# A hybrid trunk kernel on one core: S5 in stages between the weight chunks, GpSimd's work on other engines, a convolution that reads PSUM

## The chip, the cores and the metric

The kernel runs on one core of a Trainium2 chip. The metric is the device time of one execution in microseconds, lower is better. The engines are called TensorE (PE in the rows; PEld is its weight load), VectorE (DVE), ScalarE (ACT), GpSimd (POOL) and SyncE (SP). Before the change three runs took 1272.61, 1277.6 and 1278.52 us.

## What is computed

Two layers over 272 tokens (16 learned ones and 256 of the input) of width 1024. In each, one projection feeds four parallel causal mixers of width 512, whose outputs are merged by gates and followed by a squared-ReLU MLP:

```python
for l in range(DEPTH):
    proj = rms_norm(h, norm_pre_mix[l]) @ w_in[l]
    # retention (rotary q, k), S5, SSD (with a causal convolution of 4 taps), HGRN2
    y_ret, y_s5, y_ssd, y_hg = mixers(split(proj))
    mixed = sum(sigmoid(gate_n) * (y_n @ w_branch[l, n])) @ w_out[l]
    h = h + rms_norm(mixed, norm_post_mix[l])
    m = square(relu(rms_norm(h, norm_pre_mlp[l]) @ w_up[l])) @ w_down[l]
    h = h + rms_norm(m, norm_post_mlp[l])
```

The S5 mixer, with complex state of 64 for each of 32 groups of 16 channels:

```python
x_t = ab * x_{t-1} + bb @ u_t                 # complex, diagonal ab
y = gelu(real(c @ x) + d_skip * u)            # 512 channels
a, gt = split(y @ glu_w + glu_b); out = a * sigmoid(gt)
```

## The kernel before

Activations lie with channels on the partitions and tokens along the row (272 wide; the second layer's last parts 256). All large weights come as 336 chunks of 128x1024 in the order of `ORDER`, 168 a layer. `chunk` takes the next one: SyncE loads it into `wst`, ScalarE rounds it to `whi` (L325), VectorE makes the rest `wlo` (L327). `gemm` gives 24 matmuls a chunk: whi by the high half of the activation (L344), whi by its low half (L345), wlo by the high half (L347), into PSUM banks `g` (three). The other PSUM banks are `ma`, `mb` (two each) and `mc` (one).

Each engine works through its queue in order. The order is made before the run by a planner that simulates the program with times of its own and gives each engine the ready instruction of the highest priority: program order, moved ahead inside `high_priority` (a chunk's two halves by 400 places). `issue_after(x)` queues what is traced inside it behind x on x's engine.

A layer's order: HGRN2's projections (chunks 0 to 11) and its attention, the SSD's convolution inputs (12 to 19) and attention, S5's input (20 to 23), then the gates and branches: HGRN2's gate (24), gates (28), SSD's gate z (36), HGRN2's branch (40), SSD's gates (44), the rotary q and k (52), v (56), SSD's branch (60), retention's gate (64), two sets of gates (68), the GLU of S5 (84), two branches (88), the output projection (96), the MLP (104).

S5 runs in four blocks of 128 channels. For each, `s5_prep` loads 256 KB (`s5a`), builds the input matrices (`s5g`) and two output matrices (`s5b` on VectorE, `s5c` on GpSimd) by products of 512 elements (L1011 to L1013), and a table of powers (`s5e`, `s5_table`, six products of 288 elements on GpSimd). TensorE makes the direct term with 32-wide weights over 128 columns (`kd`, L1042 and L1043) and turns the input matrices (`bt`). `s5_run` multiplies by 128-wide weights over 68 columns (L1109), scales (L1115 to L1120), runs two recurrences (L1128), scales back (L1132 to L1137), multiplies again (L1143, L1146) and adds the skip term (L1139, L1148). After each second block `s5_out` applies the activation and puts rows in their places with 16 copies of 32 partitions on ScalarE and VectorE (L1160, L1162). Every S5 tile has one buffer.

`ret_in` copies q and k out of PSUM, loads the rotary tables `rot`, and lets GpSimd form four products of 32 partitions (L1496), one of 128 (L1497) and two sums. `hgrn_in` forms the forget gate on VectorE (L1201) and the key on GpSimd (L1202). In `ssd_in` the convolution copies a chunk to SBUF and then does three multiply-adds on VectorE (L1405).

Of the kernel before, what the change touches and what calls it, by code (L numbers as in the profile page):

```python
# [9 lines left out]
F32 = mybir.dt.float32  # L10
# [223 lines left out]
class Net:  # L234
    def __init__(self, ctx, tc, io, dbg=None):
# [170 lines left out]
    def layer(self, l):  # L406
# [45 lines left out]
        s5y = self.s5(l, self.s5_in(l, u_all))  # L452
# [17 lines left out]
        s5y = self.glu(l, s5y, (8, 2), sl)  # L470
# [306 lines left out]
    def scalars(self):  # L777
# [55 lines left out]
    def s5_params(self):  # L833
# [89 lines left out]
        cmul(*P(3), *P(2), *P(1))  # L923
        cmul(*P(4), *P(2), *P(2))
# [18 lines left out]
        for s in (2, 1, 0):  # L943
            cmul(c5[:, 0, s], c5[:, 1, s], cR, cI, *P(3 - s))
# [50 lines left out]
    def s5_prep(self, l, b, after=None):  # L995
# [31 lines left out]
        outer(g, self.pw[:, :, 1:5], R4[:, 2:4], cx[1][:, :, 1:5], view(tab2), 1)  # L1027
# [52 lines left out]
    def s5(self, l, W):  # L1080
        yf = self.slot(6, [128, 4, 68, 4])
        for b in range(4):
            Y = self.cmy[:, 2:4].rearrange("p a (q c) -> p (a q) c", q=4)
            if l and b == 0:
                prep = self.ahead
            else:
                fs, prep = self.s5_prep(l, b, self.decay if l and b == 1 else self.begin)
                for f in fs:
                    f()
            self.s5_run(l, b, W, prep, Y[:, 4 * (b % 2):4 * (b % 2) + 4])  # L1090
            if b % 2:
                self.s5_out(b - 1, Y, yf)
# [459 lines left out]
```

## Time and profile before

| | |
|---|---|
| profiled execution | 1277.68 us |
| its span, first to last instruction | 1275.9 us |
| median of three runs | 1277.6 us |
| TensorE busy | 1216.1 us (95%) |
| VectorE busy | 893.0 us (70%) |
| ScalarE busy | 694.2 us (54%) |
| GpSimd busy | 411.0 us (32%) |
| mean granted TensorE clock | 0.980 of 2.4 GHz |

The shares are means over stages that differ: what a stage is worth is read from its own stretch. In layer 0 the S5 blocks lie mainly between 165 and 290 us, in layer 1 between 805 and 945 us.

### The profile page before, as it was taken

What the parts mean: (1) busy time and instruction counts of PE and PEld (TensorE: products, weight loads), DVE (VectorE), ACT (ScalarE), POOL (GpSimd) and SP (SyncE); (2) the same over time, 40 slices, a digit from 0 to 9 for tenths busy, and PEclk for the clock granted to TensorE, in tenths of its full rate; (3) what the DMA queues carried; (4) which work ended last, traced back from release to release, by engine and by line L of the source; (5) the groups of instructions that cost most, each with busy time, mean ns of one, the idle gap of its engine ahead of it and who ended that gap; (6) DMA issues with size and microseconds to landing.
All of it is one profiled execution on the core that took longest, in us unless ns stands there. A gap on an engine that the chain in (4) does not pass through costs nothing.

```text
span 1275.9 us, 24312 instructions
## 1 busy us (share of the span) xinstructions
PE 1216.1 (95%) x9534; PEld 1174.6 (92%) x9534; DVE 893.0 (70%) x1480; ACT 694.2 (54%) x1219; POOL 411.0 (32%) x422
## 2 busy tenths in 40 slices
PE   8999998879999989999989999988999998999997
PEld 7999897879999989999979998987999998999996
DVE  8999989885637675544468995898656487655444
ACT  7446746443745665544455558354647546665442
POOL 2452467668002142200024333575170031322001
PEclk9999999989999989999989999998999998999998
DMA  6423232344354535555434332333444553555552
GB/s 238 160 98 104 101 123 99 108 136 145 135 175 173 176 110 178 173 175 178 170 108 143 126 123 97 123 111 114 146 150 149 184 179 136 169 188 189 182 184 98
DMA packets 53187, 186.69 MB, mean 146 GB/s; under 512 B 6096, under 2 KB 7248, under 8 KB 53072
## 3 DMA queue, kind: packets, MB, share of 16 engines
q1 hardware_dynamic: 50480, 179.40, 41.2%
q10 hardware_dynamic: 2592, 5.74, 1.4%
q8 instruction: 75, 1.23, 0.4%
q14 instruction: 40, 0.33, 0.1%
HBM read 184.06 MB, written 1.05 MB: 145 GB/s over the span
## 4 chain that ended last, share of the span: by engine, by line
PE 76%; DVE 13%; issue 4%; POOL 3%; ACT 2%; DMA 1%; SPq 0%; DVEq 0%; ACTq 0%; POOLq 0%
PE g L347 22%; PE g L344 22%; PE g L345 22%; DVE wlo L327 3%; PE mb L726 1%; PE ma L1263 1%; PE mb L717 1%; POOL S L1496 1%; DVE h L604 1%; DMA s5a<-in_bc 1%; DVE big_npom L601 1%; DVE s5a L1012 1%; ACT whi L325 1%; PE ma L726 1%; PE mb L1109 1%
## 5 line engine op out<-in xcount | busy, mean ns | idle before, releaser
L327 DVE TENSOR_TENSOR wlo<-wst,whi 128x1024 fp32r<-128x1024 f32 x336 | 438.5, 1306 | 259.1 <-PE g L347 220.8
L325 ACT ACTIVATE whi<-wst 128x1024 fp32r<-128x1024 f32 x336 | 355.8, 1060 | 365.3 <-PE g L345 287.6
L347 PE MATMUL g<-xh_u,wlo 128*128 128x272 f32 (+1 forms) x1024 | 299.7, 294 | 16.0 <-DVE wlo L327 15.8
L344 PE MATMUL g<-xh_u,whi 128*128 128x272 f32 (+1 forms) x1024 | 299.5, 293 | 0.6 <-ACT early L1068 0.4
L345 PE MATMUL g<-xl_u,whi 128*128 128x272 f32 (+1 forms) x1024 | 297.8, 291 | 0.0
L344 PE MATMUL g<-S,whi 128*128 128x272 f32 (+1 forms) x832 | 236.0, 288 | 4.6 <-ACT S L541 4.1
L347 PE MATMUL g<-S,wlo 128*128 128x272 f32 (+1 forms) x808 | 230.0, 288 | 1.7 <-DVE wlo L327 1.7
L345 PE MATMUL g<-S,whi 128*128 128x272 f32 (+1 forms) x768 | 220.4, 289 | 2.2 <-DVE S L552 1.9
L347 PEld LDWEIGHTS g<-xh_u,wlo 128*128 128x128 f32 x1024 | 195.7, 192 | 21.0 <-DVE wlo L327 18.2
L344 PEld LDWEIGHTS g<-xh_u,whi 128*128 128x128 f32 x1024 | 196.5, 192 | 2.6 <-ACT early L1068 0.7
L345 PEld LDWEIGHTS g<-xl_u,whi 128*128 128x128 f32 x1024 | 196.5, 192 | 1.5 <-issue 1.2
L344 PEld LDWEIGHTS g<-S,whi 128*128 128x128 f32 x832 | 157.1, 190 | 5.3 <-ACT S L541 4.5
L347 PEld LDWEIGHTS g<-S,wlo 128*128 128x128 f32 x808 | 151.9, 189 | 2.6 <-DVE wlo L327 2.2
L345 PEld LDWEIGHTS g<-S,whi 128*128 128x128 f32 x768 | 145.8, 190 | 4.1 <-DVE S L552 4.0
L345 PE MATMUL g<-xl_npm,whi 128*128 128x272 f32 (+1 forms) x512 | 147.7, 291 | 1.2 <-DVE xl_npm L552 1.2
L344 PE MATMUL g<-xh_npm,whi 128*128 128x272 f32 (+1 forms) x512 | 143.6, 289 | 2.4 <-ACT xh_npm L541 2.4
L347 PE MATMUL g<-xh_npm,wlo 128*128 128x272 f32 (+1 forms) x496 | 140.5, 288 | 0.0
L345 PEld LDWEIGHTS g<-xl_npm,whi 128*128 128x128 f32 x512 | 99.1, 193 | 1.9 <-DVE xl_npm L552 1.7
L344 PEld LDWEIGHTS g<-xh_npm,whi 128*128 128x128 f32 x512 | 96.7, 193 | 2.9 <-ACT xh_npm L541 2.9
L677 POOL TENSOR_TENSOR acc<-acc,tmp 128x272 f32<-128x272 f32 (+1 forms) x48 | 38.9, 828 | 186.0 <-DVE tmp L676 186.0
L347 PEld LDWEIGHTS g<-xh_npm,wlo 128*128 128x128 f32 x496 | 94.2, 192 | 0.2
L507 POOL TENSOR_TENSOR tmp<-tmp 128x272 f32<-128x272 f32 (+1 forms) x64 | 45.7, 714 | 137.3 <-DVE wlo L327 79.5
(377 smaller groups left out, 2184.4 us busy)
## 6 DMA issues: line engine op xcount, KB each, us to landing
wst<-in_w SPq DMA_DIRECT2D x336, 512.0 KB, 3.5
S<-in_rot ACTq DMA_DIRECT2D x4, 544.0 KB, 6.8
s5a<-in_bc ACTq DMA_DIRECT2D x8, 256.0 KB, 3.4
h<-in_h SPq DMA_DIRECT2D x4, 272.0 KB, 5.5
S<-in_ssdc ACTq DMA_DIRECT2D x2, 384.0 KB, 4.4
dtc<-in_ssdc ACTq DMA_DIRECT2D x2, 272.0 KB, 4.7
out<-h SPq DMA_DIRECT2D x2, 256.0 KB, 2.8
S<-in_lvl SPq DMA_DIRECT2D x1, 448.0 KB, 7.2
```

The lines of the kernel that those rows point to most:

```text
L325: a = nc.scalar.activation(hi, st, AF.Copy)
L327: nc.vector.tensor_tensor(out=lo, in0=st, in1=hi.bitcast(F32), op=ALU.subtract)
L344: self.nc.tensor.matmul(out, lhsT=a, rhs=r, start=st, stop=False)
L345: self.nc.tensor.matmul(out, lhsT=a, rhs=s, start=False, stop=False)
L347: end = self.nc.tensor.matmul(out, lhsT=b, rhs=r, start=False, stop=en)
L507: nc.gpsimd.tensor_tensor(out=q, in0=a, in1=a, op=ALU.mult)
L601: e.tensor_tensor(out=mw[:, k], in0=mw[:, k], in1=r, op=ALU.mult)
L604: e.tensor_tensor(out=self.h[:, k, sl], in0=self.h[:, k, sl], in1=mw[:, k], op=ALU.add)
L677: nc.gpsimd.tensor_tensor(out=a, in0=a, in1=t, op=ALU.add)
L717: nc.tensor.matmul(ps[:, c0:c0 + T - q0], lhsT=k[b, 128 * s:128 * s + 128], rhs=q[b, q0:T], start=True, stop=True)
L726: nc.tensor.matmul(out[:, t:T], lhsT=v01[s] if s < 2 else v2, rhs=P[:, p0:p0 + T - t], start=s == 0, stop=s == 2)
L1012: e.tensor_tensor(out=tmp, in0=X[1 - r], in1=F[1], op=ALU.mult)
```

## The change

S5 is cut into four stages a block: preparation, its products on TensorE (`products`), input products and recurrences (`states`), output products (`outputs`). They are traced when the chunk counter passes 24 + 10 b + 0, 3, 5, 8 of a layer, by `chunk` itself, and their matmuls are queued behind the last gemm matmul traced. The tables, the second output matrix and three operations of the run go from GpSimd to VectorE, the broadcast of the decay to ScalarE; the skip term becomes a matmul into the direct term (`dd`), and ScalarE copies the output from PSUM. `s5_out` places rows by 32 matmuls with columns of the identity; the first two blocks' half is taken early, the second just ahead of the GLU. Layer 1's first block is prepared behind layer 0's GLU, not ahead of its rotary stage. The rotary products are made by VectorE straight from PSUM, the exchange of halves is a matmul with a permutation `swap`, and the tables' load waits for z. HGRN2's gate and key are ScalarE's. The convolution reads PSUM, without the copy. The S5 constants' complex products are joined.

```diff
+S5_AT = (0, 3, 5, 8), 10
...
+        while self.stages and self.stages[0][0] <= self.wi:
+            self.stages.pop(0)[1]()
...
-        if not last:
-            idle, self.ahead = self.s5_prep(l + 1, 0)
         G = self.gates(l, B_SSD, u_sl, N, (10, 12))
-        rt = self.ret_in(l, u_all, t0)
+        rt = self.ret_in(l, u_all, t0, z[:, 0:1, 0:1])
...
-        s5y = self.glu(l, s5y, (8, 2), sl)
+        assert not self.stages
+        s5y = self.glu(l, self.s5_end(), (8, 2), sl)
+        if not last:
+            idle, self.ahead = self.s5_prep(l + 1, 0)
...
-        g = self.nc.gpsimd
+        g = self.nc.vector
...
-        outer(g, self.pw[:, :, 1:5], R4[:, 2:4], cx[1][:, :, 1:5], view(tab2), 1)
+        outer(v, self.pw[:, :, 1:5], R4[:, 2:4], cx[1][:, :, 1:5], view(tab2), 1)
...
+        dd = slot[0][:, 912:1040].rearrange("p (q x) -> p q x", q=4)
+        for q in range(4):
+            nc.scalar.activation(dd[:, q], self.c("ident")[:, 0:32], AF.Copy, scale=self.p(l, "s5d", 4 * b + q))
...
-                    nc.tensor.matmul(kp[:, q], lhsT=nb[:, q], rhs=cx[1][:, q, 0:4], start=False, stop=True)
+                    nc.tensor.matmul(kp[:, q], lhsT=nb[:, q], rhs=cx[1][:, q, 0:4], start=False, stop=False)
+                    nc.tensor.matmul(kp[:, q, 0], lhsT=self.c("ident")[:, 0:32], rhs=dd[:, q], start=False, stop=True)
...
-        yf = self.slot(6, [128, 4, 68, 4])
+        nc = self.nc
+        yf = self.slot(6, [128, 2, 68, 4])
+        Y = self.cmy[:, 2:4].rearrange("p a (q c) -> p (a q) c", q=4)
+        now = {}
+        def prep(b):
+            if l and b == 0:
+                now["fs"], now["prep"] = (), self.ahead
+            else:
+                now["fs"], now["prep"] = self.s5_prep(l, b, self.decay if l and b == 1 else self.begin)
+        def products(b):
+            for f in now["fs"]:
+                f(self.tc.issue_after(self.last.ins))
+        def states(b):
+            now["run"] = self.s5_run(l, b, W, now["prep"], Y[:, 4 * (b % 2):4 * (b % 2) + 4])
+            next(now["run"])
+        def outputs(b):
+            next(now["run"])
+            if b == 1:
+                for i, ps in enumerate(self.s5_out(Y)):
+                    nc.scalar.activation(yf[:, i], ps, AF.Copy)
+        def end():
+            gh, gl = self.slot(9, [128, 4, T], F32R), self.slot(7, [128, 4, T], F32R)
+            cs = lambda a: a.rearrange("p (c s) -> p c s", s=4)
+            for i in range(2):
+                self.split(yf[:, i], cs(gh[:, i]), cs(gl[:, i]))
+            for i, ps in enumerate(self.s5_out(Y)):
+                self.split(ps, cs(gh[:, 2 + i]), cs(gl[:, 2 + i]))
+            return gh, gl
+        self.s5_end = end
         for b in range(4):
...
+            for at, f in zip(S5_AT[0], (prep, products, states, outputs)):
+                self.stages.append((self.wi + b * S5_AT[1] + at, lambda f=f, b=b: f(b)))
...
-                nc.tensor.matmul(vp[:, q], lhsT=bi[:, r, q], rhs=W[:, 4 * b + q], start=True, stop=True)
+                with self.tc.issue_after(self.last.ins):
+                    nc.tensor.matmul(vp[:, q], lhsT=bi[:, r, q], rhs=W[:, 4 * b + q], start=True, stop=True)
...
-        g.tensor_tensor(out=a1, in0=a1, in1=a2, op=ALU.add)
+        v.tensor_tensor(out=a1, in0=a1, in1=a2, op=ALU.add)
...
-        g.tensor_scalar(out=m4, in0=self.m4[:, l, pr].unsqueeze(2).to_broadcast([128, 4, 68]), scalar1=1.0, scalar2=None,
-                        op0=ALU.mult)
+        nc.scalar.activation(m4, self.m4[:, l, pr].unsqueeze(2).to_broadcast([128, 4, 68]), AF.Copy)
...
-        g.tensor_tensor(out=a1, in0=z[0], in1=eR, op=ALU.mult)
+        v.tensor_tensor(out=a1, in0=z[0], in1=eR, op=ALU.mult)
...
-        g.tensor_tensor(out=a3, in0=z[0], in1=eI, op=ALU.mult)
+        v.tensor_tensor(out=a3, in0=z[0], in1=eI, op=ALU.mult)
...
-        du = a1
-        g.tensor_tensor(out=du, in0=W[:, pr], in1=self.p(l, "s5d")[:, pr].unsqueeze(2).to_broadcast([128, 4, 68]),
-                        op=ALU.mult)
+        yield
...
-        v.tensor_tensor(out=Y, in0=yp, in1=du, op=ALU.add)
-    def s5_out(self, b, Y, yf):
+        nc.scalar.activation(Y, yp, AF.Copy)
+        yield
...
+        out = []
+        for a in range(2):
+            ps = self.bank("mb")[:, :T].rearrange("p (s c) -> p s c", s=4)
             for s in range(4):
...
+                for q in range(4):
+                    nc.tensor.matmul(ps[32 * q:32 * q + 32, s], lhsT=self.c("ident")[:, 32 * s:32 * s + 32],
+                                     rhs=G[:, a, q], start=True, stop=True)
+            out.append(ps.rearrange("p s c -> p c s"))
+        return out
...
-            a, b = (0.5, 0.5) if l == 0 else (self.omlb[:, i:i + 1], self.lb[:, i:i + 1])
-            v.tensor_scalar(out=f, in0=f, scalar1=a, scalar2=b, op0=ALU.mult, op1=ALU.add)
-            g.tensor_scalar(out=KG[i // 2][:, i % 2], in0=f, scalar1=-1.0, scalar2=1.0, op0=ALU.mult, op1=ALU.add)
+            a, b, c = (0.5, self.c05, -0.5) if l == 0 else (self.omlb[:, i:i + 1], self.lb[:, i:i + 1],
+                                                           self.nomlb[:, i:i + 1])
+            nc.scalar.activation(KG[i // 2][:, i % 2], f, AF.Identity, scale=c, bias=a if l else self.c05)
+            nc.scalar.activation(f, f, AF.Identity, scale=a, bias=b)
...
-            x, ac, th = (slot[:, i] for i in range(3))
-            nc.scalar.activation(x, ps, AF.Copy)
...
-                v.scalar_tensor_tensor(out=ac[:, d:T], in0=x[:, 0:T - d], scalar=cw[:, 4 * i + k:4 * i + k + 1],
+                v.scalar_tensor_tensor(out=ac[:, d:T], in0=ps[:, 0:T - d], scalar=cw[:, 4 * i + k:4 * i + k + 1],
...
-        qk = self.slot(1, [128, 4, T])
+        qc, qs = self.slot(1, [128, 4, T]), self.slot(13, [128, 4, T])
+        rot = [self.slot(k, [128, 4, T]) for k in (8, 2)]
+        for i in range(2):
+            self.load_after(rot[i], self.io["rot"].rearrange("p (c k t) -> p c k t", c=2, k=4)[:, i], dep)
+        qf, k = self.slot(14, [128, 4, T]), self.kpad[1]
+        q = qf[:, 0:2]
         if t0:
-            g.memset(qk[:, 0:2, 0:t0], 0.0)
+            g.memset(qc[:, 0:2, 0:t0], 0.0)
+            g.memset(qs[:, 0:2, 0:t0], 0.0)
         for i in range(4):
             a = t0 if i < 2 else 0
             ps = self.proj(l, (O_RQ, O_RQ + 128, O_RK, O_RK + 128)[i], (u[0], u[1], slice(a, T)), T - a)
-            nc.scalar.activation(qk[:, i, a:T], ps, AF.Copy)
...
+            for x, r in ((qs, rot[1]), (qc, rot[0])):
+                nc.vector.tensor_tensor(out=x[:, i, a:T], in0=ps, in1=r[:, i, a:T], op=ALU.mult)
+            ps = self.bank()[:, :T]
+            nc.tensor.matmul(ps, lhsT=self.c("swap"), rhs=qs[:, i], start=True, stop=True)
+            nc.vector.tensor_tensor(out=q[:, i] if i < 2 else k[:, i - 2, 0:T], in0=ps, in1=qc[:, i], op=ALU.add)
```

## Rows read from the trace of the kernel before

**Rows 1.** The page: busy us (share of the span) and instructions; DMA issues.

```profile
PE 1216.1 (95%) x9534; PEld 1174.6 (92%) x9534; DVE 893.0 (70%) x1480; ACT 694.2 (54%) x1219; POOL 411.0 (32%) x422
...
S<-in_rot ACTq DMA_DIRECT2D x4, 544.0 KB, 6.8
```

**Rows 2.** Busy us (instructions) by stretch: PE, PEld, DVE, ACT, POOL; PEclk, DMA.

```profile
20.00:165.00 145.00, 141.99 (x1115) 133.23 (x1113) 142.78 (x409) 86.92 (x166) 64.35 (x54) 1.00 0.36 125
165.00:290.00 125.00, 108.85 (x824) 104.40 (x824) 108.70 (x153) 62.13 (x118) 81.38 (x84) 0.96 0.34 113
290.00:430.00 140.00, 140.00 (x1090) 136.86 (x1090) 83.73 (x105) 72.64 (x124) 35.57 (x30) 1.00 0.46 155
465.00:640.00 175.00, 175.00 (x1390) 175.00 (x1389) 87.45 (x97) 89.15 (x134) 19.80 (x31) 1.00 0.52 176
680.00:805.00 125.00, 123.28 (x974) 114.42 (x974) 99.57 (x182) 75.68 (x146) 42.77 (x36) 1.00 0.35 118
805.00:945.00 140.00, 127.89 (x991) 121.70 (x989) 109.44 (x152) 69.90 (x129) 84.81 (x78) 0.95 0.38 125
```

**Rows 3.** TensorE's waits, 165 to 290 us: us, times, longest.

```profile
PE g L347 <- DVE wlo L327: 9.5, 4, 2.9
PE g L344 <- DVE acc L673: 3.8, 2, 3.0
```

**Rows 4.** TensorE's waits, 805 to 945 us.

```profile
PE g L347 <- DVE wlo L327: 4.9, 3, 1.9
PE g L344 <- DVE acc L673: 3.2, 2, 2.6
```

**Rows 5.** VectorE's groups, 165 to 290 us: busy us, mean ns.

```profile
L327 DVE TENSOR_TENSOR wlo<-wst,whi 128x1024 fp32r<-128x1024 f32 x24 | 35.9, 1498 | 8.4 <-issue 5.9 <-PE g L347 2.4
...
L1011 DVE TENSOR_TENSOR s5b<-s5a,s5p 128x512 f32<-128x512 f32 x4 | 5.1, 1277 | 1.5 <-PE mb L1146 1.5
L1160 DVE COPY S<-S 32x136 f32<-32x136 f32 x16 | 4.8, 303 | 0.2
...
L1013 DVE TENSOR_TENSOR s5b<-s5b,s5a 128x512 f32<-128x512 f32 x4 | 4.5, 1114 | 0.0
L1137 DVE SCALAR_TENSOR_TENSOR s5d<-S 128x272 f32<-128x272 f32 x4 | 3.8, 941 | 0.0
...
L1134 DVE TENSOR_TENSOR s5d<-S 128x272 f32<-128x272 f32 x4 | 3.3, 832 | 0.0
...
L1128 DVE TENSOR_TENSOR_SCAN s5b<-S 128x272 f32<-128x272 f32 x4 | 2.9, 714 | 0.0
```

**Rows 6.** VectorE's groups, 465 to 640 us.

```profile
L327 DVE TENSOR_TENSOR wlo<-wst,whi 128x1024 fp32r<-128x1024 f32 x58 | 71.1, 1225 | 52.4 <-PE g L347 49.9 <-issue 1.4
L364 DVE TENSOR_TENSOR S<-tmp,S 128x272 fp32r<-128x272 f32 x28 | 12.8, 458 | 31.5 <-ACT S L362 31.4
```

**Rows 7.** Single source lines: duration ns min/median/max, first and last start.

```profile
L1013 DVE TENSOR_TENSOR s5b<-s5b,s5a x8: 675/1142/1290, 158.1 to 885.6; 128x512 f32<-128x512 f32 x8
...
L1116 DVE TENSOR_TENSOR S<-mb,s5e x8: 428/433/442, 175.8 to 888.2; 128x272 f32<-128x272 f32 x8
...
L1447 DVE SCALAR_TENSOR_TENSOR S<-S,half,mb x8: 484/489/498, 142.1 to 805.8; 128x272 f32<-128x272 f32 x8
...
L1405 DVE SCALAR_TENSOR_TENSOR S<-S,half x48: 477/484/1125, 60.9 to 758.0; 128x269 f32<-128x269 f32 x16, 128x270 f32<-128x270 f32 x16, 128x271 f32<-128x271 f32 x16
```

**Rows 8.** GpSimd's groups over the whole span.

```profile
L1496 POOL TENSOR_TENSOR S<-S,S 32x1088 f32<-32x1088 f32 x8 | 26.4, 3294 | 31.5 <-issue 22.7 <-ACT S L1489 8.5
...
L987 POOL TENSOR_TENSOR s5e<-s5ea,s5eb 128x288 f32<-128x288 f32 x8 | 8.6, 1074 | 9.4 <-DVE S L1136 8.5 <-DVE s5ea L845 0.9
```

**Rows 9.** The chain that ended last: start us, us, what.

```profile
163.71 0.22 PE mc L1042 x2
...
246.00 0.89 PE mb L1109 x8
```

**Rows 10.** ScalarE's table loads ahead of S5's activation, durations as in rows 7.

```profile
L1154 ACT ACT_TABLE_LOAD  x3: 1283/1283/1283, 216.4 to 903.5; - x3
```

More of the change, by code (lines that the diff above doesn't have):

```diff
@@ L71 @@
 _n = 0
-for _name, _w in (("ident", 128), ("ones", 128), ("cen", 128), ("m432", 432), ("he", 1), ("ho", 1), ("le", 1), ("lo", 1),
+for _name, _w in (("ident", 128), ("ones", 128), ("cen", 128), ("swap", 128), ("m432", 432), ("he", 1), ("ho", 1), ("le", 1), ("lo", 1),
                   ("rh", 1), ("rl", 1), ("r1", 1)):
@@ L105, in shape_constants @@
     put("cen", np.eye(128) - 1.0 / 128)
+    put("swap", np.eye(128)[p ^ 32])
     t = np.arange(T)
@@ L260, in __init__ @@
         self.hold = {}
+        self.stages = []
+        self.last = None
     def slot(self, k, shape, dt=F32):
@@ L351, in gemm @@
                                             start=False, stop=stop and k == n - 1)
+        self.last = end
         return end
@@ L922, in s5_params @@
         cmul(*P(2), *P(1), *P(1))
-        cmul(*P(3), *P(2), *P(1))
-        cmul(*P(4), *P(2), *P(2))
+        sh = [128, 2, DEPTH, 16]
+        d = d4[:, 0:64].rearrange("p (i l q) -> p i l q", i=2, l=DEPTH)
+        cmul(pw[:, 0, 3:5], pw[:, 1, 3:5], pw[:, 0, 1:3], pw[:, 1, 1:3],
+             *[x.unsqueeze(1).to_broadcast(sh) for x in P(2)])
         c5 = self.cp.tile([128, 2, 4, DEPTH, 16], F32, name="s5c")
@@ L942, in s5_params @@
         tt(cI, cI, inv, ALU.mult)
-        for s in (2, 1, 0):
-            cmul(c5[:, 0, s], c5[:, 1, s], cR, cI, *P(3 - s))
+        sh = [128, 3, DEPTH, 16]
+        d = d4[:, 0:96].rearrange("p (i l q) -> p i l q", i=3, l=DEPTH)
+        cmul(c5[:, 0, 0:3], c5[:, 1, 0:3], *[pw[:, r, 3:0:-1] for r in range(2)],
+             *[x.unsqueeze(1).to_broadcast(sh) for x in (cR, cI)])
+        d = new()
         self.eb = self.cp.tile([128, 2, DEPTH, 16, 8], F32, name="s5eb")
@@ L1080, in s5 @@
     def s5(self, l, W):
-        yf = self.slot(6, [128, 4, 68, 4])
-        for b in range(4):
[L1083 to L1092, printed above, removed]
-        yf = yf.rearrange("p a c s -> p a (c s)")
-        gh, gl = self.slot(9, [128, 4, T], F32R), self.slot(7, [128, 4, T], F32R)
-        for i in range(4):
-            self.split(yf[:, i], gh[:, i], gl[:, i])
-        return gh, gl
+        nc = self.nc
[27 more added lines that the diff above has]
+        self.s5_end = end
+        for b in range(4):
+            for at, f in zip(S5_AT[0], (prep, products, states, outputs)):
+                self.stages.append((self.wi + b * S5_AT[1] + at, lambda f=f, b=b: f(b)))
     def s5_run(self, l, b, W, prep, Y):
@@ L1155, in s5_out @@
         G = Y.rearrange("p (a q c) -> p a q c", a=2, q=4)
-        for q in range(4):
+        out = []
+        for a in range(2):
+            ps = self.bank("mb")[:, :T].rearrange("p (s c) -> p s c", s=4)
             for s in range(4):
-                o, i = yf[32 * q:32 * q + 32, b:b + 2, :, s], G[32 * s:32 * s + 32, :, q, :]
-                if q % 2:
-                    nc.vector.tensor_copy(o, i)
-                else:
-                    nc.scalar.activation(o, i, AF.Copy)
+                for q in range(4):
[3 more added lines that the diff above has]
+        return out
     def glu(self, l, x, ks, sl):
@@ L1399, in ssd_in @@
             slot = self.slot(13 + i % 2, [128, 4, T])
-            x, ac, th = (slot[:, i] for i in range(3))
-            nc.scalar.activation(x, ps, AF.Copy)
+            ac, th = (slot[:, i] for i in range(2))
             nc.scalar.activation(ac, ps, AF.Identity, scale=cw[:, 4 * i + 3:4 * i + 4], bias=cb[:, i:i + 1])
```

28 lines of the change are left out of this document (11 added, 17 removed).

## The prediction, before the run

> **What bounds the kernel now.** I read the page first, then the busy times by stretch, then TensorE's waits in two of the stretches, then single groups for prices. The page says TensorE: 1216.1 us busy of a span of 1275.9 [rows 1]. A pure matmul stretch shows the pace: 1390 matmuls in 175 us, 0.126 us each, so a chunk of 24 takes 3.0 us [rows 2]. The program is therefore bound by the sum of TensorE's work, plus what TensorE loses. The stretches say where it loses. From 290 to 430 us it is busy for all of 140.00 us. From 165 to 290 us (layer 0, where S5 runs) it is busy for 108.85 of 125, at a mean granted clock of 0.96; from 805 to 945 us (the same part of layer 1) 127.89 of 140, at 0.95 [rows 2]. These two hold 16.2 + 12.1 = 28.3 us of idle time. Between the two clock levels, 0.96 means that 8% of 125 us, 10 us, ran at 1.2 GHz in place of 2.4, which costs half of it, 5.0 us; 0.95 in 140 us costs 7.0. Together 40.3 us: that is the prize.
>
> Why it is lost: the longest waits in both stretches are for the low half of a weight chunk (wlo, L327) and for VectorE's gated product that frees a bank (L673) [rows 3, 4]. Both are VectorE's. It is busy for 108.70 of the first stretch's 125 us, with GpSimd at 81.38 [rows 2]. The reader should see two things. A full VectorE alone does not make TensorE wait: from 20 to 165 us VectorE is busy for 142.78 of 145 and TensorE for 141.99 [rows 2]. And the operations on VectorE are stretched in the S5 part: one wlo takes 1.498 us there, against 1.225 us where GpSimd is nearly idle [rows 5, 6]; a 512-wide product of two SBUF operands has a median of 1.142 us and a least of 0.675 (L1013), while a product that reads PSUM stays within 0.428 to 0.442 (L1116) [rows 7]. I read this as GpSimd and VectorE holding each other up where both read SBUF. The queues are ordered beforehand from a plan's times, and a wlo that is a quarter longer than usual arrives late.
>
> **The change part by part.**
>
> *GpSimd's work goes away.* Of a block it gave the 6 table products (L987: 1.074 us each) and the 3 of the second output matrix, sums and products of the scan; of a layer, four quarter-height rotary products (L1496: 3.294 us each) and the sums behind them [rows 8]. None of it ended a TensorE wait of any length in these stretches, except through VectorE, so its removal is worth what VectorE gets back.
>
> *What VectorE gets, layer 0.* I price at the rows where GpSimd is quiet: 0.458 us for 272 elements with two SBUF operands [rows 6], so 0.485 for 288; 0.68 for 512; 0.433 from PSUM [rows 7]. Tables 4 x 6 x 0.485 = 11.6; second output matrix 4 x 3 x 0.68 = 8.2; scan 4 x 3 x 0.458 = 5.5; rotary 4 x 3 x 0.433 = 5.2. Sum 30.5. Off go four sums of the output (1.7) and 16 placing copies at 0.303 (4.8) [rows 5]: net +24.0. Preparing layer 1's first block moves behind the GLU: nine 512-wide products at about 0.9 (between 0.68 and the 1.277 of [rows 5]), so -8. Net +16. In layer 1 only three blocks are prepared: 8.7 + 6.1 + 5.5 + 5.2 - 6.5 = +19.
>
> *What VectorE gets back.* 24 wlo x (1.498 - 1.225) = 6.6; the three groups of four 512-wide products at 1.277 to 1.114 (the first and last of the three are shown) against 0.68: 6.1; L1137 and L1134 at 0.941 and 0.832 against 0.458: 3.4 [rows 5, 6]. Sum 16.1, other groups uncounted. So VectorE ends up about as full as it was, but with even durations. From below the relief is nothing, if the stretching has another cause; from above it is the whole sum and the uncounted groups.
>
> *The new places.* A block has ten chunks, 30.3 us of matmuls. VectorE needs about 17.9 us for a block by the prices above (twelve products of 512, six of 288, two recurrences at 0.714 [rows 5], and 12 operations of 272) and 10 x 1.225 for the wlo: 30.2 in all, before gates and merges. So a block won't keep its ten chunks. That costs nothing while it slides: after the last stage (chunk 62) there are 22 chunks to the GLU, 66 us, in a stretch where VectorE is busy for 83.73 of 140 [rows 2]. The S5 matmuls are queued behind the last gemm matmul; where their operand is late, the next chunks' matmuls stand behind them. I leave 10 of the 40.3 us lost: the two stretches ahead, with VectorE full but little GpSimd, lose (145 - 141.99) + (125 - 123.28) = 4.7 us of 270 at a full clock [rows 2], which is 4 us for these two. Bounds: 4 and all 40.3. I take 10, near the low end, as the same queue with even durations is what those rows show. Back: -30.
>
> *TensorE's new work.* 128 placing matmuls (32 weights wide, 68 columns), 8 swaps (272 columns), 32 for the skip (32 columns). Matmuls of 128 columns with 32-wide weights follow each other by 0.11 us (x2 0.22), so 68 columns take 0.058 us; 68 columns behind 128-wide weights take 0.111 (x8 0.89) [rows 9]. The shape is that of the first row: 128 x 0.058 = 7.5. The swaps by columns 8 x 0.234 = 1.9, the skip 32 x 0.028 = 0.9. Sum +10.3; at 0.111 for each small one 14.2 + 1.9 + 3.6 = 19.7. From below 4.7, if four matmuls to four groups of output rows overlapped fully, for which I have no row. [...]
>
> *The convolution.* 24 operations of a layer read PSUM in place of an SBUF copy. Median 0.489 with one PSUM operand (L1447), 0.484 with SBUF alone (L1405) [rows 7]: no loss. The eight removed copies are ScalarE's, which is at 54% [rows 1] and not in TensorE's way. [...]
>
> *Smaller ones.* HGRN's blend goes from VectorE and GpSimd to ScalarE, the S5 constants take 12 VectorE operations in place of 30, the prepared block moves. Between 20 and 165 us and between 680 and 805 us that can return at most the 4.7 us that TensorE idles there; I take -2. The rotary tables (544 KB, 6.8 us to landing [rows 1]) must now be there before the first q chunk leaves PSUM; they wait for the gate z, and twelve chunks, 36 us, lie between: nothing, and 7 us a layer without that cover. GLU: the second half of S5's output is activated and placed only ahead of it. The first nine matmuls cover one copy, not two: 1 us a layer, +2; from above that is a rival.
>
> **Sum**, against the profiled execution's 1277.68 us (span 1275.9, and 1.8 around it; the median of the three is 1277.6): 1277.7 - 30 + 10.3 - 2 + 2 = 1258.0 us.
>
> **Rivals.** *The waits only shrink by half* (0.15): VectorE stays as full as before by my own sum, the wlo still comes late behind S5's new operations, and the queueing behind gemm matmuls changes little, since the plan orders by priority anyway. Back 20, TensorE's work at 15, GLU 2: 1274.7, no measurable change. For it: VectorE at 108.70 of 125 [rows 2]. Against it: 20 to 165 us.
>
> *VectorE becomes the bound, slower* (0.09): the place is the S5 stretch of each layer. Of the relief only a third comes (about 6 a layer), so +10 and +13 us of VectorE's work go into a queue that TensorE follows, and no wait is returned: 1277.7 + 23 + 10.3 = 1311; 1290 if half of the surplus slides behind chunk 62. It decides where the relief falls below the +16 and +19 of new work and S5 doesn't slide. Against it: least durations of 0.675 that stand in the trace.
>
> *The GLU waits for S5* (0.04): if the last block slides to chunk 84, the activation (with a table load of 1.283 [rows 10]), 32 placing matmuls at 0.111 and two copies stand bare: 6 us a layer, and 3 of half clock behind it, half of what each stretch loses by that now. 1258 + 18 = 1276. It decides when S5's slide passes 66 us.
>
> The forecast has 0.72, with its own range from 1277.7 - 36 + 5 - 2 = 1245 to 1277.7 - 20 + 13 = 1271. For 8 in 10 I go to 1243 (the uncounted relief) and 1277 (the first rival). Half a per cent, 1271.2 to 1284.0, is about what a measurement of this kernel can tell. Faster: the forecast's 0.72 and a little of the first rival, 0.74; same 0.15; slower 0.11.
>
> **What would show it.** In the changed profile: wlo near 1.23 us in S5's stretches and the least and median of L1013's products alike; GpSimd far below its 411.0 us [rows 1]; TensorE's wait for wlo, 9.5 + 4.9 us there now [rows 3, 4], below 5; granted clock 0.98 or more; 128 placing matmuls near 0.06 us apart; no idle time ahead of the GLU. The forecast is wrong if wlo stays at 1.4 or more, if S5's own matmuls end long waits, or if the placing takes 0.11 us each with the waits still there.

## The result, and the profile after

The changed kernel takes 1263.97 us, the median of four runs (1261.48 to 1265.03), against 1277.07 (1272.61 to 1278.52) for the kernel before on the same chip. The ratio is 0.99, with a 95% interval of 0.9871 to 0.9929. It is faster, by 13 us in place of the 20 that the forecast of 1258 had. The profiled execution took 1265.03 us.

The page of the changed kernel first, its span and the line of busy times: GpSimd fell from 411.0 us to 213.4 and VectorE from 893.0 to 869.7, while TensorE's busy time grew by 6.3 us.

```profile
span 1263.2 us, 24851 instructions
PE 1222.4 (97%) x9870; PEld 1184.1 (94%) x9870; DVE 869.7 (69%) x1536; ACT 695.1 (55%) x1232; POOL 213.4 (17%) x289
```

The busy times by stretch of the changed kernel, to be laid beside [rows 2]. The one stretch from 20 to 165 us is cut in three here.

```profile
core 0: us, PE busy (x) PEld busy (x) DVE busy (x) ACT busy (x) POOL busy (x), PEclk, DMA share, GB/s
20.00:60.00 40.00, 39.28 (x316) 38.21 (x316) 39.97 (x150) 24.60 (x48) 11.03 (x13) 1.00 0.51 165
60.00:115.00 55.00, 45.90 (x345) 43.54 (x343) 55.00 (x158) 18.81 (x32) 16.56 (x17) 0.88 0.24 77
115.00:165.00 50.00, 50.00 (x380) 45.43 (x380) 42.09 (x87) 40.80 (x85) 16.83 (x12) 1.00 0.32 98
165.00:290.00 125.00, 123.97 (x1058) 121.15 (x1058) 102.93 (x181) 65.87 (x128) 6.55 (x20) 1.00 0.46 144
290.00:430.00 140.00, 139.99 (x1120) 135.54 (x1119) 86.63 (x121) 73.08 (x129) 21.54 (x28) 1.00 0.47 151
680.00:805.00 125.00, 123.24 (x989) 115.69 (x988) 98.37 (x185) 72.67 (x137) 37.94 (x40) 1.00 0.36 114
805.00:945.00 140.00, 137.48 (x1171) 132.67 (x1170) 102.81 (x183) 75.54 (x147) 14.78 (x29) 0.99 0.44 137
```

Two things are to be seen. In the two S5 stretches TensorE now idles for 1.0 and 2.5 us, where it idled for 16.2 and 12.1, and its clock is 1.00 and 0.99 where it was 0.96 and 0.95. And a hole has opened where there was none: from 60 to 115 us TensorE idles for 9.1 us, at a granted clock of 0.88. The kernel before shows there:

```profile
60.00:115.00 55.00, 53.79 (x444) 51.27 (x444) 54.88 (x131) 27.99 (x52) 25.72 (x19) 1.00 0.32 108
```

What TensorE waited for in the changed kernel, in 60 to 115 us (the first two rows), 165 to 290 (the third) and 805 to 945 (the fourth); columns: the tile and line that waited, what released it, us in total, times, the longest. They answer to [rows 3, 4].

```profile
PE ma L1311 <- DVE S L1374: 6.5, 2, 3.8
PE ma L1329 <- DVE S L1374: 2.2, 1, 2.2
...
PE mb L1205 <- ACT S L1198: 0.9, 1, 0.9
...
PE g L353 <- DVE wlo L333: 2.3, 1, 2.3
```

The waits for wlo, 9.5 and 4.9 us before, are gone in layer 0 and 2.3 us in layer 1. The new waits are HGRN2's: its attention matmuls (L1311, L1329) wait for products on VectorE (L1374), and VectorE is busy for all 55.00 us there.

Single groups on VectorE in the changed kernel, 165 to 290 us: the wlo (L333), which answers to [rows 5], and the last 512-wide product of the input matrices (L1030); the third row is that product in the kernel before, in the same stretch.

```profile
L333 DVE TENSOR_TENSOR wlo<-wst,whi 128x1024 fp32r<-128x1024 f32 x30 | 36.6, 1220 | 10.1 <-issue 6.3 <-PE g L353 3.8
L1030 DVE TENSOR_TENSOR s5g<-s5g,s5a 128x512 f32<-128x512 f32 x8 | 5.5, 685 | 0.0
...
L1013 DVE TENSOR_TENSOR s5g<-s5g,s5a 128x512 f32<-128x512 f32 x8 | 7.6, 945 | 0.0
```

And single lines over the whole run, ns least, median, most: the product that was L1013, the convolution that now reads PSUM, and the matmuls that place S5's rows. They answer to [rows 7].

```profile
L1030 DVE TENSOR_TENSOR s5b<-s5b,s5a x8: 674/683/685, 127.1 to 885.5; 128x512 f32<-128x512 f32 x8
...
L1452 DVE SCALAR_TENSOR_TENSOR S<-g,half,S x48: 476/481/496, 60.8 to 749.2; 128x269 f32<-128x269 f32 x16, 128x270 f32<-128x270 f32 x16, 128x271 f32<-128x271 f32 x16
...
L1205 PE MATMUL mb<-S,cst x256: 222/223/247, 221.8 to 963.1; 128*32 128x68 f32 x128
```

A wlo takes 1.220 us where it took 1.498, and a 512-wide product's least, median and most lie within 11 ns, where they lay between 0.675 and 1.290. What the prediction said would be seen on VectorE is there. The gain is not there in full: the first chunk of layer 0's GLU is rounded by ScalarE from 373.4 us on, against 376.3 before, that of layer 1 from 994.6 against 1007.7. Layer 1 gives 10 us, layer 0 only 3.

### The profile page after: what moved, and what is told of

It reads as the page before. It is cut to its first block, busy times and chain, and to the rows that moved or that the text cites. A ratio compares the mean times of both kernels' runs of the same rounds, so it can differ in the third digit from the quotient of the medians.

```text
span 1263.2 us, 24851 instructions
## 1 busy us (share of the span) xinstructions
PE 1222.4 (97%) x9870; PEld 1184.1 (94%) x9870; DVE 869.7 (69%) x1536; ACT 695.1 (55%) x1232; POOL 213.4 (17%) x289
## 4 chain that ended last, share of the span: by engine, by line
PE 84%; DVE 10%; ACT 3%; issue 1%; DMA 1%; SPq 0%; ACTq 0%; DVEq 0%
PE g L350 24%; PE g L353 24%; PE g L351 24%; DVE wlo L333 2%; PE mb L736 1%; PE mb L1154 1%; PE mb L1189 1%; DVE S L1320 1%; DVE h L614 1%; PE mb L727 1%; DVE S L1452 1%; PE mb L706 1%; DVE xl_npm L562 1%; PE ma L727 1%; ACT whi L331 1%
## 5 line engine op out<-in xcount | busy, mean ns | idle before, releaser
L333 DVE TENSOR_TENSOR wlo<-wst,whi 128x1024 fp32r<-128x1024 f32 x336 | 418.2, 1246 | 246.6 <-PE g L353 210.3
L350 PE MATMUL g<-xh_u,whi 128*128 128x272 f32 (+1 forms) x1024 | 299.6, 293 | 0.2
L350 PE MATMUL g<-S,whi 128*128 128x272 f32 (+1 forms) x832 | 236.3, 288 | 3.8 <-ACT S L551 3.3
L350 PEld LDWEIGHTS g<-xh_u,whi 128*128 128x128 f32 x1024 | 195.0, 190 | 2.7 <-DVE S L696 0.6
L350 PEld LDWEIGHTS g<-S,whi 128*128 128x128 f32 x832 | 157.2, 190 | 4.6 <-ACT S L551 3.6
L350 PE MATMUL g<-xh_npm,whi 128*128 128x272 f32 (+1 forms) x512 | 143.7, 288 | 2.4 <-ACT xh_npm L551 2.4
L350 PEld LDWEIGHTS g<-xh_npm,whi 128*128 128x128 f32 x512 | 96.4, 191 | 2.7 <-ACT xh_npm L551 2.5
L371 DVE TENSOR_TENSOR S<-tmp,S 128x272 fp32r<-128x272 f32 (+1 forms) x56 | 25.1, 449 | 61.2 <-ACT S L369 61.2
```

The source lines that it names most:

```text
L333: nc.vector.tensor_tensor(out=lo, in0=st, in1=hi.bitcast(F32), op=ALU.subtract)
L350: self.nc.tensor.matmul(out, lhsT=a, rhs=r, start=st, stop=False)
L371: nc.vector.tensor_tensor(out=lo, in0=src, in1=hi.bitcast(F32), op=ALU.subtract)
```

## The experiments

They ran in three rounds, each on a chip of its own and beside the kernel before, whose median was between 1276.9 and 1277.5 us; the ratios are against that. All compute the whole of the reference. Three questions were open: what took the gain back between 60 and 115 us, whether the stages matter, and which part of the removed GpSimd work makes the gain.

### What opened the hole: convolution, gate or constants

**The copy back (e1).** The changed kernel, with the convolution's copy to SBUF.

```diff
-            ac, th = (slot[:, i] for i in range(2))
+            x, ac, th = (slot[:, i] for i in range(3))
+            nc.scalar.activation(x, ps, AF.Copy)
...
-                v.scalar_tensor_tensor(out=ac[:, d:T], in0=ps[:, 0:T - d], scalar=cw[:, 4 * i + k:4 * i + k + 1],
+                v.scalar_tensor_tensor(out=ac[:, d:T], in0=x[:, 0:T - d], scalar=cw[:, 4 * i + k:4 * i + k + 1],
```

> The changed kernel with the convolution's copy to SBUF put back (ScalarE copies each chunk out of PSUM, VectorE's three operations read the copy). In the changed kernel TensorE is idle for 9.8 us between 20 and 165 us (135.18 of 145 busy, granted clock 0.95), where the kernel before lost 3.0 at a full clock. Theory A (VectorE's S5 constants and first preparation now run between 60 and 110 us, inside HGRN2's chain, and hold it up): nothing changes, 1264 us within 3, idle 8 to 11 us in that stretch. Theory B (without the copy each of the three gemm banks is held until VectorE has read it three times, and VectorE is full there, so TensorE can't run ahead): idle below 5 us at a clock of 0.99 or more, 1253 us within 3.

1261.35 us, ratio 0.9875 (0.9859 to 0.989). From 60 to 115 us TensorE is busy for 48.83 us in place of 45.90, at a clock of 0.94. Some of the hole seems to be the convolution's, but the idle time from 20 to 165 us, 6.9, lies between the two that were expected, and the interval overlaps that of the changed kernel: by itself this settles little.

**The gate back (e2).** The changed kernel, with HGRN2's forget gate on VectorE and the key on GpSimd.

```diff
-            nc.scalar.activation(KG[i // 2][:, i % 2], f, AF.Identity, scale=c, bias=a if l else self.c05)
-            nc.scalar.activation(f, f, AF.Identity, scale=a, bias=b)
+            b = b if l else 0.5
+            v.tensor_scalar(out=f, in0=f, scalar1=a, scalar2=b, op0=ALU.mult, op1=ALU.add)
+            g.tensor_scalar(out=KG[i // 2][:, i % 2], in0=f, scalar1=-1.0, scalar2=1.0, op0=ALU.mult, op1=ALU.add)
```

> The changed kernel with HGRN2's forget gate back on VectorE and its key back on GpSimd, as before. Theories A and B: VectorE gets 8 operations of 0.3 to 0.4 us more ahead of HGRN2, so 1264 to 1267 us, idle of TensorE in 20 to 165 us still 8 us or more. Theory C (the earlier gate lets the plan start HGRN2's chain earlier, so that the plan differs from the chip there): idle below 5 us, 1253 to 1257 us.

1264.0 us, 0.9899 (0.988 to 0.9918); 46.72 us busy from 60 to 115. The gate is not the cause. TensorE's longest waits in this stretch are other ones here: the next chunk's first matmuls (L350) wait for a bank that the convolution (L1453) still reads.

```profile
PE g L350 <- DVE S L1453: 5.0, 2, 4.3
```

**The constants held back (e3).** In the changed kernel S5's constants (small products, L857) and the first block's 512-wide products, which need them, run among HGRN2's products. They did so before too, but less of them in this place. The constants alone between 60 and 115 us, VectorE's busy time before (L845) and after (L857):

```profile
60.00:115.00 55.00, 5.17 (x20) 1.00 0.32 108
...
60.00:115.00 55.00, 10.44 (x48) 0.88 0.24 77
```

The 512-wide products there take 5.3 us in place of 2.5. Here the constants are queued behind HGRN2's last operation on VectorE, and the products come later with them.

```diff
-            self.s5_params()
+            with self.tc.issue_after(self.hgend.ins):
+                self.s5_params()
...
-        nc.vector.tensor_tensor(out=y, in0=y, in1=r, op=ALU.mult)
+        self.hgend = nc.vector.tensor_tensor(out=y, in0=y, in1=r, op=ALU.mult)
```

> The changed kernel with the S5 constants queued on VectorE behind HGRN2's last VectorE operation in layer 0, so that the first block's preparation (which needs them) comes behind it as well. Theory A: HGRN2's products no longer wait 2 to 4 us for VectorE, TensorE's idle time in 20 to 165 us falls from 9.8 below 5 us at a clock of 0.99 or more, 1253 us within 4. Theory B: the idle time stays at 8 us or more, and S5 comes later: 1264 to 1268 us.

1258.14 us, 0.9844 (0.9825 to 0.9863), outside the changed kernel's interval. TensorE is busy for 51.66 of the 55 us at a full clock, though for 46.16 of the next 50. S5's early work is one cause; what the constants and the preparation have of it each was not separated.

**The constants apart (e12).** Perhaps it was the joining of their products. The changed kernel, with single complex products as before.

```diff
+        cmul(*P(3), *P(2), *P(1))
+        cmul(*P(4), *P(2), *P(2))
...
+        for s in (2, 1, 0):
+            cmul(c5[:, 0, s], c5[:, 1, s], cR, cI, *P(3 - s))
```

> The changed kernel with the S5 constants' complex products apart again (30 VectorE operations in place of 12). If the joined products are what brings the constants and the first preparation into HGRN2's chain: TensorE's idle time in 60 to 115 us falls from 9.1 below 4 us and the time to 1254 to 1259 us. If they only shorten the list: idle time as it was, 1264 to 1268 us.

1266.7 us, 0.9914 (0.9898 to 0.9931), not told apart from the changed kernel. TensorE is busy for 48.14 us from 60 to 115 at 0.88, and for 47.45 of the next 50. The constants take 5.69 us there, about as before the change, and the 512-wide products 5.3, and the hole has not closed: the joining moved the constants, but neither it nor their larger share makes the hole by itself.

**The convolution alone (e5).** The kernel before, with only the convolution reading PSUM.

```diff
-            x, ac, th = (slot[:, i] for i in range(3))
-            nc.scalar.activation(x, ps, AF.Copy)
+            ac, th = (slot[:, i] for i in range(2))
...
-                v.scalar_tensor_tensor(out=ac[:, d:T], in0=x[:, 0:T - d], scalar=cw[:, 4 * i + k:4 * i + k + 1],
+                v.scalar_tensor_tensor(out=ac[:, d:T], in0=ps[:, 0:T - d], scalar=cw[:, 4 * i + k:4 * i + k + 1],
```

> The kernel before with one edit: the convolution reads PSUM and the copy is gone. Theory B (banks held while VectorE is full): TensorE's idle time between 60 and 115 us, 1.2 us in the kernel before, rises above 3 us, 1278 to 1283 us. Theory A' (a price per operation alone): 0.489 us a multiply-add in place of 0.579, 4 us of VectorE over both layers, idle time as before, 1273 to 1277 us.

1283.68 us, 1.0052 (1.0035 to 1.007): slower by 6.6 us by the ratio, 6.2 by the medians. The single operation is no dearer, even cheaper: 24 of the convolution's operations between 60 and 165 us take 11.3 us where they took 13.7. The price lies elsewhere. The timeline of this kernel, one channel chunk's reads of its bank (start, us, engine, line): ScalarE's scaled read, then VectorE's three.

```profile
64.88 0.56 ACT L1401 ACTIVATE S<-g,half 128x272 f32<-128x272 f32 x1
...
68.00 0.48 DVE L1404 SCALAR_TENSOR_TENSOR S<-g,half,S 128x269 f32<-128x269 f32 x1
72.22 0.46 DVE L1404 SCALAR_TENSOR_TENSOR S<-g,half,S 128x270 f32<-128x270 f32 x1
...
76.73 0.49 DVE L1404 SCALAR_TENSOR_TENSOR S<-g,half,S 128x271 f32<-128x271 f32 x1
```

The bank of the same channel chunk in the kernel before, by the same view: the copy and the scaled read.

```profile
64.38 0.38 ACT L1401 ACTIVATE S<-g 128x272 f32<-128x272 f32 x1
64.66 0.57 ACT L1402 ACTIVATE S<-g,half 128x272 f32<-128x272 f32 x1
```

Before, the bank was free after 0.85 us; now it is held for 12.3, as each read waits its turn on an engine that is busy for 54.45 of 55 us. The `gemm` banks are three. That the hold is what costs the time is likely and not shown: in this kernel no wait of TensorE between 60 and 165 us names the convolution (the longest in total, 4.1 us, is for HGRN2's products), and the planner's order changed with the edit: S5's early work takes 10.5 us of VectorE from 60 to 115, where it took 7.7. In e2 such a wait is seen.

**Copy and hold together (e10).** The changed kernel with the first and the third edit.

```diff
+            nc.scalar.activation(x, ps, AF.Copy)
...
+            with self.tc.issue_after(self.hgend.ins):
+                self.s5_params()
```

> The changed kernel with its stages, the convolution's copy put back and the S5 constants behind HGRN2. With the stages gone as well it took 1249.7 us. If the stages by themselves cost or bring nothing: 1249.7 within 2. If they cost what the run without them seemed to show: 1252 to 1254. If they bring something once VectorE is free of the other two: below 1247.

1251.55 us, 0.9804 (0.9789 to 0.9818). The hole is closed; the stretches of this kernel:

```profile
60.00:115.00 55.00, 54.53 (x451) 52.37 (x450) 52.99 (x111) 26.56 (x53) 22.52 (x18) 1.00 0.35 111
115.00:165.00 50.00, 49.77 (x360) 44.24 (x359) 33.84 (x98) 36.49 (x70) 10.73 (x8) 1.00 0.33 107
165.00:290.00 125.00, 125.00 (x1045) 120.20 (x1045) 117.43 (x304) 63.10 (x121) 17.62 (x25) 1.00 0.46 147
```

Against the hold alone the copy is worth 6.6 us here by the medians and 5.1 by the ratios, about as much as in the kernel before. The two edits are 12.4 us together, where alone they gave 2.6 and 5.8: each is worth more once the other is made.

### Whether the stages matter

**Unstaged (e4).** The changed kernel, with all of S5 traced at chunk 24.

```diff
-S5_AT = (0, 3, 5, 8), 10
+S5_AT = (0, 0, 0, 0), 0
```

> The changed kernel with all four stages of all four S5 blocks traced at once at chunk 24, so only GpSimd's work stays moved. If the even durations on VectorE are what removed the waits: TensorE idle below 3 us in the layer 0 stretch 165 to 290 us, time within 4 us of 1264. If the stages are: 5 to 12 us idle there and as much in layer 1, 1272 to 1282 us.

1260.97 us, 0.9869 (0.9852 to 0.9885): not slower. TensorE is busy for 123.83 of 125 and 139.30 of 140 us in the S5 stretches.

**All three (e7).** Copy, hold and no stages: the edits of e1, e3 and e4 on the changed kernel.

```diff
+            nc.scalar.activation(x, ps, AF.Copy)
...
+                self.s5_params()
...
+S5_AT = (0, 0, 0, 0), 0
```

> The changed kernel with three edits together: the convolution's copy back, the S5 constants behind HGRN2, and all S5 stages traced at once. Singly they gave 1261.4, 1258.1 and 1261.0 against 1264.0. If each acts on its own: 1252 us within 3. If all three act on the same loss, TensorE's 9 us in 60 to 115 us of layer 0: 1256 to 1259, as the best alone.

1249.71 us, 0.979 (0.9762 to 0.9819), the same as with the stages. In neither pair do they bring anything that could be measured: without them the medians are 3.0 and 1.8 us lower, and from 805 to 945 us TensorE idles for 0.7 and 0.9 us, where with them it idles for 2.5. Whether they would help where GpSimd still stretches VectorE was not run.

### Which GpSimd work makes the gain

**Tables back (e6).** The changed kernel, with the power tables and the second output matrix on GpSimd again.

```diff
-        g = self.nc.vector
+        g = self.nc.gpsimd
...
-        outer(v, self.pw[:, :, 1:5], R4[:, 2:4], cx[1][:, :, 1:5], view(tab2), 1)
+        outer(g, self.pw[:, :, 1:5], R4[:, 2:4], cx[1][:, :, 1:5], view(tab2), 1)
```

> The changed kernel with the S5 tables and the second output matrix back on GpSimd (VectorE does 9 operations a block less, GpSimd some 11 us a block more), all else as changed. If GpSimd's SBUF traffic is what stretched VectorE: the mean wlo in 165 to 290 us is 1.35 us or more (1.498 before, near 1.23 in the changed kernel), TensorE idles there for 6 us or more, 1269 to 1277 us. If the moves only rearranged the queues: wlo below 1.3, VectorE less busy, 1264 us within 4.

1267.98 us, 0.9932 (0.991 to 0.9953). wlo is stretched again, to 1.337 us from 165 to 290 and 1.374 from 805 to 945; yet TensorE idles there for 1.9 and 2.4 us only, where 6 or more were expected. VectorE has 94.98 us to do in the first, not 102.93. Here the stretching alone doesn't make TensorE wait. The intervals overlap, so a price is not settled.

```profile
165.00:290.00 125.00, 123.06 (x1053) 120.04 (x1053) 94.98 (x145) 65.05 (x124) 41.46 (x46) 1.00 0.44 141
...
L333 DVE TENSOR_TENSOR wlo<-wst,whi 128x1024 fp32r<-128x1024 f32 x31 | 41.4, 1337 | 11.1 <-issue 6.3 <-PE g L353 4.8
```

**S5 alone (e8).** The kernel before, with S5's operations moved from GpSimd to VectorE and nothing else.

```diff
-        g = self.nc.gpsimd
+        g = self.nc.vector
...
-        outer(g, self.pw[:, :, 1:5], R4[:, 2:4], cx[1][:, :, 1:5], view(tab2), 1)
+        outer(v, self.pw[:, :, 1:5], R4[:, 2:4], cx[1][:, :, 1:5], view(tab2), 1)
...
-        g.tensor_tensor(out=a1, in0=a1, in1=a2, op=ALU.add)
+        v.tensor_tensor(out=a1, in0=a1, in1=a2, op=ALU.add)
```

(and likewise the two products by eR and eI)

> The kernel before with one part alone: the tables, the second output matrix and the three sums and products of the run on VectorE in place of GpSimd; no stages, placing by copies, rotary and convolution as before. If even durations on VectorE are the gain: mean wlo in 165 to 290 us below 1.3 us, TensorE's idle time there down from 16.2 to 6 us or less, 1262 to 1268 us. If VectorE's added 25 us a layer bind, as the rival had it: idle time 16 us or more and 1280 us or more.

1266.99 us, 0.9928 (0.9907 to 0.9949). The time is as expected, the idle time is not: TensorE still idles for 11.5 us of the first stretch, 9.2 of them in one wait for wlo. And that although a wlo takes 1.216 us there on average: the mean says nothing of this wait.

```profile
PE g L347 <- DVE wlo L327: 9.2, 1, 9.2
...
L327 DVE TENSOR_TENSOR wlo<-wst,whi 128x1024 fp32r<-128x1024 f32 x26 | 31.5, 1216 | 0.8 <-issue 0.6 <-ACT s5f L1059 0.2
```

The timeline of this kernel just ahead of it, VectorE's rows and the one of GpSimd:

```profile
270.77 2.77 DVE L1011 TENSOR_TENSOR s5c<-s5a,s5p 128x512 f32<-128x512 f32 x1
273.46 3.01 DVE L1012 TENSOR_TENSOR s5d<-s5a,s5p 128x512 f32<-128x512 f32 x1
276.40 2.73 DVE L992 TENSOR_TENSOR s5e<-s5e 128x288 f32<-128x288 f32 x1
279.05 2.96 DVE L1013 TENSOR_TENSOR s5b<-s5b,s5a 128x512 f32<-128x512 f32 x1
...
270.45 11.01 POOL L1496 TENSOR_TENSOR S<-S,S 32x1088 f32<-32x1088 f32 x4
```

While GpSimd works at its four quarter-height rotary products, VectorE's operations take 2.7 to 3.0 us, the 512-wide ones four times their 0.68. What is left is the rotary stage.

**Rotary alone (e9).** The kernel before, with only the rotary stage of the changed kernel (products from PSUM on VectorE, the swap on TensorE).

```diff
-        rt = self.ret_in(l, u_all, t0)
+        rt = self.ret_in(l, u_all, t0, z[:, 0:1, 0:1])
```

(with the changed `ret_in` and the permutation as a constant)

> The kernel before with one part alone: the rotary products on VectorE straight from PSUM and the exchange of halves as a matmul, with the tables' load behind z; S5 as before. With S5 alone moved, four rotary products on GpSimd stretched single VectorE operations to 2.7 to 3 us and TensorE waited 9.2 and 5.7 us for a wlo there. If that is a cost of the rotary by itself: 1268 to 1274 us. If in the kernel before it lies where TensorE has work anyway: 1276 to 1279 us.

1279.62 us over ten runs, 1.0018 (1.0007 to 1.0029): no gain, rather a loss of 2 us. wlo is at 1.399 and 1.355 us, and TensorE idles for 16.7 and 13.0 us of the two stretches: S5's share on GpSimd holds VectorE up as before. With the tables and the second output matrix alone on GpSimd, in the changed kernel, there was no such idle time (e6); what makes the difference, the operations of the run on GpSimd or another of the changed kernel's parts, no run separates.

**Both (e11).** The kernel before with these two edits; no stages, no placing matmuls, the convolution with its copy, the constants as they were.

```diff
-        g = self.nc.gpsimd
+        g = self.nc.vector
...
-        rt = self.ret_in(l, u_all, t0)
+        rt = self.ret_in(l, u_all, t0, z[:, 0:1, 0:1])
```

> The kernel before with two parts: the five S5 operations on VectorE and the rotary products on VectorE and TensorE; no stages, placing by copies, convolution with its copy. If GpSimd's hold on VectorE is the whole of the gain: wlo below 1.25 us in 165 to 290 us, TensorE's idle time there below 4 us, 1250 to 1257 us, better than the change. If the stages, the placing by matmuls or the other moves are needed: 1261 us or more, idle time in that stretch above 8 us.

1247.77 us (1246.49 to 1248.51), 0.977 (0.9755 to 0.9784): the fastest, 2.3% below the kernel before and 16 us below the changed one. Its S5 stretches and its wlo from 165 to 290 us:

```profile
165.00:290.00 125.00, 123.41 (x967) 117.20 (x963) 116.34 (x221) 68.90 (x130) 26.40 (x36) 1.00 0.41 131
805.00:945.00 140.00, 136.59 (x1106) 130.73 (x1106) 110.39 (x201) 82.37 (x151) 29.33 (x36) 1.00 0.43 140
...
L328 DVE TENSOR_TENSOR wlo<-wst,whi 128x1024 fp32r<-128x1024 f32 x28 | 34.1, 1218 | 1.7 <-PE g L348 0.9 <-issue 0.6 <-ACT s5f L1060 0.2
```

VectorE is even fuller than before (116.34 us, where it was 108.70), and TensorE idles for 1.6 us there, where it idled for 16.2: the two parts are enough, without the others. The parts alone give -9.2 and +2.3 us by their ratios, together -29.4. Each leaves the other's hold in place.

## Why the prediction was right, and where it failed

**What bounds the kernel, and why TensorE idled: right in the main.** The rows fit GpSimd and VectorE holding each other up where both read SBUF: in the kernel before, a 512-wide VectorE product of SBUF operands takes 0.675 to 1.290 us (L1013) and a table product of GpSimd 0.683 to 1.533 (L987), while VectorE's gated product with an operand in PSUM (L673) stays within 0.406 to 0.426, also at 207.39 and 211.95 us, where a table product runs beside it. The prediction's row for PSUM (L1116) says less: a product of GpSimd runs beside only one of its eight. With both parts of GpSimd's work gone, wlo is at 1.220 us and nearly all of the waits are gone; with either half left in the kernel before (e8, e9), most of them stay. That VectorE need not grow lighter was right too, as e11 shows best. One link is not shown as it was written: that "a wlo that is a quarter longer than usual arrives late". In e6 it is a tenth longer (1.337) and TensorE hardly waits; in e8 it has its usual length, and TensorE waits 9.2 us for it behind operations that are stretched fourfold and more. Nor was it quite so that GpSimd's work ended no TensorE wait by itself: in the kernel before, two waits of 1.3 and 0.9 us in these stretches ended on its second output matrix (s5c).

**The -30 of the S5 stretches: too small.** Idle time fell from 28.3 to 3.5 us. Counted as in the prediction, half clock costs 1.4 where it cost 12.0. That is 35 us back, nearer to the bound of 36 than to 30. In the kernel before, windows of 2 us from 165 to 290 us read a clock of 1.00 or 0.50, and between them only where it changes. There 24 steps of 272-column matmuls from 279.61 us on, at 0.50, take 5.44 us, 0.227 each, against 0.126 at 1.00. That is 1.8 times, so the count by halves is about a tenth too high. 272 columns in 0.227 us are 1.2 a ns: that, and its double at the full share, is all that a run shows of the prediction's 1.2 and 2.4 GHz.

**TensorE's new work, 10.3: its rows misread, and too small.** Each of these matmuls leaves two records in the trace, and the prediction took them for two matmuls. The kernel before calls L1042 32 times (4 blocks, 4 groups, 2 layers), and its trace has 64:

```profile
L1042 PE MATMUL mc<-s5b,s5g 128*32 128x128 f32 x64 | 13.4, 293 | 0.4 <-DVE s5b L1013 0.3
```

So "x2 0.22" [rows 9] is one matmul of 128 columns, and by columns 68 take 0.117 us, not 0.058: by its own rows the prediction should have had 15.0 for the placing, 3.7 for the swaps and 1.8 for the skip, 20.5 in all. The changed kernel's first 32 placing matmuls stand together on the chain that ended last, and there they are far cheaper:

```profile
221.81 1.16 PE mb L1205 x64
```

That is 0.036 a matmul, 3.2 times less than 0.117. But of the 128, only 64 stand in such bursts. The others are strewn between gemm matmuls, 2 to 38 records at a time, and there even a single one is dear:

```profile
320.49 0.29 PE L351 MATMUL g<-xl_u,whi 128*128 128x272 f32 x1
320.71 0.31 PE L1205 MATMUL mb<-S,cst 128*32 128x68 f32 x2
320.94 0.39 PE L353 MATMUL g<-xh_u,wlo 128*128 128x272 f32 x1
321.17 0.29 PE L350 MATMUL g<-xh_u,whi 128*128 128x272 f32 x1
```

From the first to the last start are 0.68 us, where two steps of 0.126 would do: 0.43 us for one matmul. Counted so from the starts in the trace, the placing takes 2.6 us in the two bursts and 7.0 elsewhere, the swaps 3.7 (0.46 each) and the skip 1.9 (0.06 each): 15.2 us.

**GLU, +2 and its rival:** from 290 to 430 us TensorE is busy for 139.99 of 140, and from 945 to 1010 for all of 65. No GLU waits for S5. The slide behind the chunks left no idle time there, and the stages brought nothing that was measured.

**The step that failed: "Smaller ones", with "no loss" for the convolution.** It had -2 for the stretches ahead of S5. Between 60 and 115 us there are 9.1 us of idle time in place of 1.2, and at 0.88 up to 24% of 55 us at half clock, 6.6 us at most. Two things are shown to make the hole, and undoing both returns 12.4 us and closes it. The first is the convolution: I priced its operation (0.489 against 0.484; it is 0.481) and not what it holds. A bank that ScalarE freed in 0.85 us is held for some 12. The edit costs some 6 us in the kernel before and beside the hold, though only 2.6 where S5's early work is left in place; that the held bank is the way by which it costs is likely, and not shown. The second is S5's early work, constants and first preparation, inside HGRN2's chain on a full VectorE: 5.8 us by itself, 9.8 once the copy is back. I had cut the constants' operations from 30 to 12 and counted that as a gain; what I didn't ask is where the planner would put them. It now has 15.8 us of S5's work between 60 and 115, where it had 7.7. Why it brought that forward is open in part: with the products apart (e12) the constants go back to 5.7 us, but the preparation stays and so does the hole; the gate (e2) changes neither; and no run looked further.

With the measured terms the sum is 1277.7 - 35.3 + 15.2 + 12.4 = 1270.0, against 1265.0 of the profiled execution; 5.0 us are not placed. That the time fell into the forecast's own range, 1245 to 1271, is in part luck: a loss of 12.4 us that the prediction had as a gain of 2, and 5 more of new work, stand against 5 us more of relief, a GLU that cost nothing and the 5.0 that are not placed.

**The rivals.** That the waits only shrink by half is refuted by 28.3 to 3.5 us, that VectorE becomes the bound by the S5 stretches, where TensorE is busy for all but 3.5 of 265 us. The measured 1265.0 is 7 us above the forecast and 10 below the first rival's 1274.7, but not because half of the waits stayed: something else took a third of the relief back.

## What to carry to other kernels

Price an edit by what it holds as well as by how long it runs: three operations that read a PSUM bank on a full engine hold it until the last of them has had its turn, 12.3 us in e5 for 0.85 before. Before pricing from a row, count how many records of the trace one call of the program leaves; and price a short matmul where it will stand, in a burst (0.036 us here) or alone between others (0.43). Where two engines hold each other up, look at all of the contending work at once, since one half alone may show little or nothing: -9.2 and +2.3 us here, and -29.4 together. And where a planner orders the queues, see after each edit which work off the chain it has now put inside the tightest chain, and tie that work down.

## What the runs showed of the hardware

The prediction took the stretching for a mean: 0.68 us becomes some 1.1. In e8 it is one for one. GpSimd's four rotary products take 11.01 us, 2.75 each, and beside them VectorE gets through four operations, which end at 273.54, 276.47, 279.13 and 282.01 us, whether of 512 elements or of 288: each lasts about as long as the GpSimd operation that it stands beside. It is not one for one everywhere: in the kernel before, three wlo beside the same products (3.4 us each) in layer 1 take 1.88, 2.32 and 2.04 us. Beside the short operations of S5 (1.074 us [rows 8]) 512-wide products take 1.114 to 1.277 us on average [rows 5] in place of 0.68, 0.4 to 0.6 us more; beside the rotary ones they take 2.77 to 3.01, over 2 us more and four times their length, and TensorE waits 9.2 us for a wlo behind them.
